# Two transformer blocks in exact-split fp32 on one core: activations streamed as hi and lo side by side, and the delta rule run in steps between weight products

## The chip, the cores and the metric

The kernel runs on one core of one Trainium2 chip. The metric is device time in microseconds, the median of several executions. The engines are named as in the profile: PE (TensorE matmul), PEld (its weight loads), DVE (VectorE), ACT (ScalarE), POOL (GpSimd) and SP (SyncE, which issues most transfers).

## What is computed

The input is x, 256 tokens by 2048 features. Two blocks of different kinds follow each other, each with weight matrices of 2048 rows and more, in float32:

```python
# first block
h = rms_norm(x, ln1[l])
proj = h @ w_in[l]                       # 11280 columns, split below
qkv_a, beta_a, decay_a, z_a, qkv_b, gate_a, gate_b = split_columns(proj)
y_a = gated_deltanet(qkv_a, beta_a, decay_a, z_a, ...) @ w_branch_a[l]
q_b, k_b, v_b = jnp.split(qkv_b, 3, axis=-1)     # rope on q and k, then attention
y_b = moba_attention(q_b, k_b, v_b).reshape(B, S, MOBA_WIDTH) @ w_branch_b[l]
x = x + (sigmoid(gate_a) * y_a + sigmoid(gate_b) * y_b) @ w_out[l]
u = causal_dwconv(rms_norm(x, ln2[l]) @ w_up[l], ffn_conv[l], ffn_conv_bias[l])
x = x + (silu(u_gate) * u_val) @ w_down[l]
# second block
z = h @ w_in[0]                          # pool columns, and r, k, v and lora columns
x = x + concat([pool_out, rwkv_out]) @ w_out[i]
x = x + jnp.square(jax.nn.relu(h2 @ w_ffn_up[i])) @ w_ffn_down[i]
x = x + sigmoid(rms_norm(x, ple_norm[i]) @ w_ple_gate[i]) * (p[i] @ w_ple_proj[i])
```

`gated_deltanet` is a recurrence over chunks of 64 tokens for 8 heads; the second block has another of the same kind (rwkv) for 16 heads of 64.

## The kernel before

Every product is made of three: an operand is split into hi (its value in the fp32r type that PE multiplies fast) and lo (the rest), and hi by hi, lo by hi and hi by lo are summed in PSUM. `load_w` fetches 512 KB of a weight matrix (raw) on SP's queue, ACT makes hi of it (L307) and DVE lo (L308); raw, hi and lo have three buffers each. The activations lie with features on partitions (`Norm.h`, `Norm.l`, tiles xh and xl, 16 slices of 128 features by 256 tokens).

`group_steps` computes 512 output columns: for each of the 16 slices and each half of the tokens, xh or xl is the stationary operand and 512 columns of the weight stream past it:

```python
mm(p, xh, h[:, j], start=(k == 0), stop=False, skip_group_check=True)    # L331
mm(p, xl, h[:, j], start=False, stop=False, skip_group_check=True)       # L332
mm(p, xh, l[:, j], start=False, stop=last, skip_group_check=True)        # L333
```

The result has tokens on partitions. Where the next step needs features on partitions, `turned_steps` has ACT evacuate it into u, times the norm's factor r (L368), and `feature_major` turns it by eight 128 x 128 transposes on PE (L249) for 512 columns; `take` then reads the turned tile in PSUM. So are computed: gdn_proj (q, k, v of the delta rule, 6 groups of 512 columns), q and k of the attention (4 groups, after a rotation by POOL along the row), up1 (22 groups), the lora columns (288), r, k, v and the pool columns of the second block (8 groups) and up2 (16 groups). The merge in branch_b is turned too. All other products (z, the gates, v, the branches, w_out, w_down) are used with tokens on partitions.

The order within an engine is that in which the program is written, shifted by a scheduler that works from its own model of the times; each engine then takes its instructions strictly in that order. In the first block the program text runs gdn_proj(0), z_proj(0), gdn_half(0), gdn_proj(1), z_proj(1), gdn_half(1), then attention. `gdn_half` is a chain: scales (L516), `gdn_pre` (L537 to L557), `inverse16`, which passes through DRAM and gives Z, `inverse64` and the rest of the inverse (L673 to L706), and `gdn_post` for two pairs of heads (L573 to L612). In the second block the chain of rwkv yields after each step, and `run` takes a number from a hand-written table after each and pulls so many units of other projections (`fill`) into the text there; a step of a projection costs 1.8 units.

PSUM has four one-bank tiles pp for the products, two of them for a group, and four tiles ps for the rest.

## Time and profile before

| what | value |
|---|---|
| median of three runs | 2911.91 us (2908.76 to 2915.29) |
| profiled execution, its own time | 2914.03 us |
| its span, first to last instruction | 2912.3 us |
| PE busy | 2818.7 us, 97%, 14224 instructions |
| DVE busy | 1698.9 us, 58% |
| ACT busy | 1391.3 us, 48% |
| POOL busy | 162.5 us, 6% |
| mean granted clock of PE | 0.976 |
| moved by DMA | 487.72 MB, mean 167 GB/s |

A busy share counts the time in which an engine has an instruction in flight. Matmuls overlap each other, so for PE the distance between the starts of two of them tells what one costs, and its duration doesn't. The granted clock is a share of 2.4 GHz; PE has two levels, 2.4 and 1.2 GHz, and a value between them is a mean over a stretch.

### The profile page before, as it was taken

To read this page: it belongs to the slowest core of one execution; us is meant where nothing else is said; L and a number is where in the kernel's file an instruction comes from. 1 tells how busy PE (TensorE), PEld (TensorE's weight loads), DVE (VectorE), ACT (ScalarE), POOL (GpSimd) and SP (SyncE) were. 2 spreads that over 40 slices of the span, in tenths; PEclk is the share of its full clock that TensorE was granted. 3 is DMA by queue.
4 is the path that set the end of the run, shared out by engine and by line. 5 is a ranking of instruction groups with operands and counts; after the bars stand their busy time and mean duration, and the time that the engine had idled before them with its cause. 6 is when DMAs were issued, how large, how long until landed. Compare 5 with 4: busy or idle time off the path is not lost.

```text
span 2912.3 us, 37683 instructions
## 1 busy us (share of the span) xinstructions
PE 2818.7 (97%) x14224; PEld 2298.8 (79%) x14224; DVE 1698.9 (58%) x2599; ACT 1391.3 (48%) x2062; POOL 162.5 (6%) x225
## 2 busy tenths in 40 slices
PE   9988989999999999999999999979999999999997
PEld 7867868888888888888887677766888888888886
DVE  6556656555556664665566595765645444454555
ACT  6535445444455544554455644423543443434454
POOL 0000100000000000000001031120010000100001
PEclk9988989999999999999999999988999999999999
DMA  7543535666566666666655454342565656666554
GB/s 214 168 121 102 164 102 170 180 190 185 182 184 186 184 187 189 187 182 187 203 179 176 133 141 131 104 123 73 152 186 187 188 184 188 185 187 201 182 181 152
DMA packets 281499, 487.72 MB, mean 167 GB/s; under 512 B 36442, under 2 KB 51813, under 8 KB 281317
## 3 DMA queue, kind: packets, MB, share of 16 engines
q1 hardware_dynamic: 280533, 482.94, 55.8%
q8 instruction: 111, 1.82, 0.3%
q10 hardware_dynamic: 608, 2.11, 0.2%
q14 instruction: 71, 0.58, 0.1%
q0 software_dynamic: 176, 0.27, 0.1%
HBM read 479.22 MB, written 6.03 MB: 167 GB/s over the span
## 4 chain that ended last, share of the span: by engine, by line
PE 90%; DVE 5%; DMA 2%; issue 1%; POOL 1%; ACT 1%; SPq 0%; ACTq 0%; DVEq 0%; POOLq 0%
PE pp L331 27%; PE pp L333 27%; PE pp L332 27%; PE ps L249 2%; DVE lo L308 2%; DMA s<-Ei 0%; PE ps L680 0%; DVE L L1082 0%; POOL X L664 0%; DMA Z<-s 0%; PE ps L1148 0%; PE ps L1150 0%; POOL pool L1231 0%; DMA raw<-in_w_in_dram 0%; PE ps L1160 0%
## 5 line engine op out<-in xcount | busy, mean ns | idle before, releaser
L308 DVE TENSOR_TENSOR lo<-raw,hi 128x1024 fp32r<-128x1024 f32 (+2 forms) x905 | 1113.4, 1231 | 982.3 <-ACT hi L307 927.1
L307 ACT ACTIVATE hi<-raw 128x1024 fp32r<-128x1024 f32 (+2 forms) x905 | 953.3, 1054 | 1097.4 <-PE pp L332 996.7
L331 PE MATMUL pp<-hi,xh 128*128 128x512 f32 (+1 forms) x2368 | 924.0, 390 | 2.6 <-ACT hi L307 2.0
L332 PE MATMUL pp<-hi,xl 128*128 128x512 f32 (+1 forms) x2368 | 923.2, 390 | 0.0
L333 PE MATMUL pp<-lo,xh 128*128 128x512 f32 (+1 forms) x2368 | 865.3, 390 | 8.1 <-DVE lo L308 7.9
L333 PEld LDWEIGHTS pp<-lo,xh 128*128 128x128 f32 x2368 | 445.4, 189 | 99.5 <-DVE lo L308 11.9
L331 PEld LDWEIGHTS pp<-hi,xh 128*128 128x128 f32 x2368 | 447.0, 189 | 94.2 <-issue 3.0
L332 PEld LDWEIGHTS pp<-hi,xl 128*128 128x128 f32 x2368 | 447.1, 189 | 88.7 <-issue 2.3
L332 PE MATMUL pp<-hi,hid 128*128 128x512 f32 x864 | 342.4, 397 | 0.0
L331 PE MATMUL pp<-hi,hid 128*128 128x512 f32 x864 | 342.1, 397 | 0.0
L333 PE MATMUL pp<-lo,hid 128*128 128x512 f32 x864 | 313.2, 397 | 0.0
L332 PEld LDWEIGHTS pp<-hi,hid 128*128 128x128 f32 x864 | 162.6, 188 | 39.6 <-DVE hid L380 0.5
L331 PEld LDWEIGHTS pp<-hi,hid 128*128 128x128 f32 x864 | 162.6, 188 | 38.9
L333 PEld LDWEIGHTS pp<-lo,hid 128*128 128x128 f32 x864 | 162.5, 188 | 38.7 <-DVE lo L308 0.2
L895 DVE SCALAR_TENSOR_TENSOR cva<-ps,PT,cva 128x255 f32<-128x255 f32 (+1 forms) x176 | 79.4, 477 | 2.1 <-ACT cva L892 1.0
L368 ACT ACTIVATE u<-pp,rstd 128x512 f32<-128x512 f32 (+1 forms) x74 | 49.9, 680 | 56.5 <-PE pp L333 49.7
L249 PE MATMUL ps<-C,u 128*128 128x128 f32 x486 | 73.8, 280 | 0.6 <-ACT u L368 0.6
L1322 POOL TENSOR_TENSOR u<-u 128x512 f32<-128x512 f32 x32 | 40.6, 1269 | 595.6 <-ACT u L1321 595.6
L249 PEld LDWEIGHTS ps<-C,u 128*128 128x128 f32 x486 | 61.7, 144 | 14.5 <-ACT u L368 1.0
L270 POOL TENSOR_TENSOR junk<-x,rows 128x512 f32<-128x512 f32 x8 | 12.3, 1536 | 1087.9 <-ACT junk L267 1087.9
L864 DVE TENSOR_TENSOR x<-x,pp 128x512 f32<-128x512 f32 x96 | 65.2, 686 | 4.8 <-PE pp L333 3.6
L331 PE MATMUL pp<-hi,mh 128*128 128x512 f32 x128 | 51.0, 398 | 0.0
(426 smaller groups left out, 2322.2 us busy)
## 6 DMA issues: line engine op xcount, KB each, us to landing
raw<-in_w_in_dram SPq DMA_DIRECT2D x240, 512.0 KB
raw<-in_w_up_dram SPq DMA_DIRECT2D x176, 512.0 KB
raw<-in_w_ffn_up_dram SPq DMA_DIRECT2D x128, 512.0 KB
raw<-in_w_ffn_down_dram SPq DMA_DIRECT2D x128, 512.0 KB
raw<-in_w_down_dram SPq DMA_DIRECT2D x88, 512.0 KB
raw<-in_w_out_dram SPq DMA_DIRECT2D x64, 512.0 KB
raw<-in_w_ple_gate_dram SPq DMA_DIRECT2D x32, 512.0 KB
raw<-in_w_branch_a_dram SPq DMA_DIRECT2D x16, 512.0 KB
```

The lines of the kernel that those rows point to most:

```text
L249: nc.tensor.transpose(p[:w, m - m0, i * 128:(i + 1) * 128], src[:, i, 128 * m:128 * m + w], ident)
L270: nc.gpsimd.tensor_tensor(out=y, in0=s, in1=self.w2[j], op=ALU.mult)
L307: act(h, r, AF.Copy)
L308: tt(out=l, in0=r, in1=h.bitcast(F32), op=ALU.subtract)
L331: mm(p, xh, h[:, j], start=(k == 0), stop=False, skip_group_check=True)
L332: mm(p, xl, h[:, j], start=False, stop=False, skip_group_check=True)
L333: mm(p, xh, l[:, j], start=False, stop=last, skip_group_check=True)
L368: act(u[:, i, :ncol], p, AF.Copy, scale=r()[:, i:i + 1])
L864: tt(out=s, in0=s, in1=p, op=ALU.add)
L895: stt(a[:, s:], p[:, :T - s], prm("ffn_conv", 88 * j + f), a[:, s:], ALU.mult, ALU.add)
L1322: nc.gpsimd.tensor_tensor(out=u[:, i], in0=u[:, i], in1=u[:, i], op=ALU.mult)
```

## The change

It has two parts. First, `wide_steps` takes the place of `turned_steps` and of `group_fm_steps`: the weight is the stationary operand, and hi and lo of the activations lie side by side in one tile xhl, so that one matmul streams 512 columns (256 tokens of hi, 256 of lo) past 128 columns of the weight's hi, and a second one streams the 256 columns of hi past the weight's lo. The result has features on partitions, 256 of them in one pass; raw holds four slices of 256 columns in place of two of 512. At the end of a pass ACT copies the part that came from lo to z, DVE adds the other part from PSUM and multiplies by the factor, which `spread` has turned into a row for all partitions. The rotation of q and k works along partitions, by a shuffle on DVE and three POOL operations. up2 squares on DVE instead of POOL. The pp tiles are two of two banks.

Second, `Fill` holds projections that are yet to be computed. The steps of `gdn_half` and of the attention heads yield numbers of units, and so many units of products are put between them: z and the second half's projections beside the first half of the delta rule, the attention's projections beside the second, gates and branch_a beside the heads. The second block's `pull` uses the same class: a step of `wide_steps` counts 1.0, one of `group_steps` 2.0 for 512 columns; the table of numbers is as it was.

```diff
-    pp = ctx.enter_context(tc.tile_pool(name="pp", bufs=4, space=bass.MemoryType.PSUM))
+    pp = ctx.enter_context(tc.tile_pool(name="pp", bufs=2, space=bass.MemoryType.PSUM))
...
+    def spread(col):
+
+        p2 = psum()
+        for i in range(2):
+            nc.tensor.transpose(p2[:, i * 128:(i + 1) * 128], col[:, i:i + 1].to_broadcast([128, 128]), ident)
+        rb = tm("rstd", T, bufs=1)
+        act(rb, p2[:, :T], AF.Copy)
+        return rb
...
-            self.h = cpool.tile([128, KT, T], F32R, tag="xh", name=nm("xh"))
-            self.l = cpool.tile([128, KT, T], F32R, tag="xl", name=nm("xl"))
+            self.hl = cpool.tile([128, KT, 2, T], F32R, tag="xhl", name=nm("xhl"))
...
+                        mm(P[:w, m].rearrange("p a b -> p (a b)"), h[:, j, f], x2.rearrange("p a b -> p (a b)"),
+                           start=(k == 0), stop=False, skip_group_check=True)
+                        mm(P[:w, m, 0], l[:, j, f], x2[:, 0], start=False, stop=last, skip_group_check=True)
+                        if not (last and m == len(ws) - 1):
+                            yield 1.0
+            w, nw = ws[0], len(ws)
+            z = tm("z", (2, T), bufs=2)[:w, :nw]
+
+            act(z, P[:w, :nw, 1], AF.Copy)
+            tt(out=z, in0=P[:w, :nw, 0], in1=z, op=ALU.add)
+            if r is not None:
+                tt(out=z, in0=z, in1=r()[:w].unsqueeze(1).to_broadcast([w, nw, T]), op=ALU.mult)
+            for m in range(nw):
+                take(o0 // 128 + m, z[:, m])
+            yield 1.0
...
+        Z = inverse16([p[0][:, 0] for p in pre], 2)
+        yield 55
+        for _ in rounds(gdn_inverse(pre[m:m + 2], Z[:, m:m + 2]) for m in (0, 2)):
+            yield 6
         for m in (0, 2):
-            lockstep(gdn_post(4 * half + m + i, sc, pre[m + i]) for i in range(2))
+            for _ in rounds(gdn_post(4 * half + m + i, sc, pre[m + i]) for i in range(2)):
+                yield 5
...
+    z0, z1, g1, a0, a1 = z_proj(0), z_proj(1), gdn_proj(1), attn_proj(0), attn_proj(1)
+    fills.add(z0, g1, z1)
+    fills.pull(30)
+    fills.between(gdn_half(0))
+    fills.upto(z1)
+    fills.add(a0, a1)
+    fills.between(gdn_half(1))
+    fills.upto(a0)
+    fills.between(rounds(attn_head(h) for h in (0, 1)))
+    fills.between(rounds(attn_head(h) for h in (2, 3)))
+    fills.upto(a1)
+    ba = [branch_a(j) for j in range(4)]
+    fills.add(*ba)
+    fills.between(rounds(attn_head(h) for h in (4, 5)))
+    fills.between(rounds(attn_head(h) for h in (6, 7)))
+    fills.upto(ba[3])
...
+        def ev(m, p):
+            stt(p, p, 0.0, p, ALU.max, ALU.mult)
+            split(hh[:, m], hl[:, m], p)
+
+        wide(w_up, 512 * i, 512, xs, lambda: r5, ev)
```

In the changed file the products of `group_steps` are L345 to L347, those of `wide_steps` L373 and L375, lo is L320, and the chain of the delta rule has moved down: L673 is L729 there, L700 and L706 are L756 and L762, L573 is L622, L612 is L661.

On PE, in an up projection of the first block, products and the transposes of the group before stood so (pp is the group's PSUM tile, C the identity, u the evacuated group):

```order
L331 MATMUL pp_11622<-hi_11644,xh_6034 128x512
L332 MATMUL pp_11622<-hi_11644,xl_6035 128x512
L249 MATMUL ps_11582<-C_84,u_11433 128x128
L249 MATMUL ps_11601<-C_84,u_11433 128x128
L333 MATMUL pp_11622<-lo_11645,xh_6034 128x512
...
L331 MATMUL pp_11622<-hi_11662,xh_6034 128x512
L249 MATMUL ps_11582<-C_84,u_11433 128x128 x3
L249 MATMUL ps_11601<-C_84,u_11433 128x128 x3
L332 MATMUL pp_11622<-hi_11662,xl_6035 128x512
```

At the seam of two passes of the same projection there is now:

```order
L373 MATMUL pp_12328<-xhl_6318,hi_12397 128x512
L375 MATMUL pp_12328<-xhl_6318,lo_12398 128x256
L373 MATMUL pp_12436<-xhl_6318,hi_12439 128x512
L375 MATMUL pp_12436<-xhl_6318,lo_12440 128x256
...
L373 MATMUL pp_12436<-xhl_6318,hi_12461 128x512
L375 MATMUL pp_12436<-xhl_6318,lo_12462 128x256
```

The transposes are gone from PE's queue, and products of 512 and 256 columns alternate.

On DVE, at the end of the second group of an up projection (cva is the convolution's sum, sgq the gate), before:

```order
L308 TENSOR_TENSOR lo_10732<-raw_10729,hi_10731 128x1024
L895 SCALAR_TENSOR_TENSOR cva_10622<-ps_10617,PT_81,cva_10622 128x255
L895 SCALAR_TENSOR_TENSOR cva_10622<-ps_10617,PT_81,cva_10622 128x254
L906 TENSOR_TENSOR cva_10622<-cva_10622,sgq_10286 128x256
L308 TENSOR_TENSOR lo_10750<-raw_10747,hi_10749 128x1024
```

and now:

```order
L320 TENSOR_TENSOR lo_12376<-raw_12373,hi_12375 128x1024
L382 TENSOR_TENSOR z_12310<-pp_12221,z_12310 128x512
L384 TENSOR_TENSOR z_12310<-z_12310,rstd_7019 128x512
L320 TENSOR_TENSOR lo_12398<-raw_12395,hi_12397 128x1024
L958 SCALAR_TENSOR_TENSOR cva_12314<-z_12310,PT_81,cva_12314 128x255
L958 SCALAR_TENSOR_TENSOR cva_12321<-z_12310,PT_81,cva_12321 128x255
L958 SCALAR_TENSOR_TENSOR cva_12314<-z_12310,PT_81,cva_12314 128x254
L958 SCALAR_TENSOR_TENSOR cva_12321<-z_12310,PT_81,cva_12321 128x254
L969 TENSOR_TENSOR cva_12314<-cva_12314,sgq_12012 128x256
L320 TENSOR_TENSOR lo_12440<-raw_12437,hi_12439 128x1024
```

The two operations on z are new there, and stand between two lo.

On PE, at the delta rule's first half, from the end of the inverse to the first pair's post, before (aq, c, d, f and e are the chain's own tiles):

```order
L706 MATMUL ps_1461<-aq_1166,ivp_1452 64x64 x2
L706 MATMUL ps_1461<-aq_1195,ivp_1452 64x64 x2
L706 MATMUL ps_1468<-aq_1224,ivp_1459 64x64 x2
L706 MATMUL ps_1468<-aq_1253,ivp_1459 64x64 x2
L573 MATMUL ps_1475<-c_1175,aq_1166 128x128
L573 MATMUL ps_1479<-c_1204,aq_1195 128x128
L578 MATMUL ps_1483<-d_1477,f_1173 128x128
```

and now in the first half:

```order
L762 MATMUL ps_1821<-aq_1227,ivp_1794 64x64 x2
L375 MATMUL pp_2846<-xhl_96,lo_2894 128x256
L373 MATMUL pp_2846<-xhl_96,hi_2915 128x512
L762 MATMUL ps_1828<-aq_1268,ivp_1801 64x64 x2
...
L375 MATMUL pp_2951<-xhl_96,lo_2955 128x256
L373 MATMUL pp_2951<-xhl_96,hi_2954 128x512
L622 MATMUL ps_1882<-c_1198,aq_1189 128x128
L622 MATMUL ps_1886<-c_1236,aq_1227 128x128
```

and in the second half (oah is the first half's result, which branch_a multiplies):

```order
L347 MATMUL pp_4567<-lo_4601,oah_98 128x512
L729 MATMUL ps_3038<-X_3016,aq_2617 64x64 x4
...
L762 MATMUL ps_3276<-aq_2701,ivp_3249 64x64 x2
L762 MATMUL ps_3276<-aq_2746,ivp_3249 64x64 x2
L622 MATMUL ps_3328<-c_2626,aq_2617 128x128
L622 MATMUL ps_3332<-c_2671,aq_2662 128x128
L627 MATMUL ps_3348<-d_3330,f_2624 128x128
```

In the first half products now stand between the steps of the chain; in the second they stand ahead of it, and the inverse and most of post follow each other without them.

## Rows read from the trace of the kernel before

**Rows 1.** The page: busy time, share and instructions of each engine, and the chain that ended last by engine and line.

```profile
PE 2818.7 (97%) x14224; PEld 2298.8 (79%) x14224; DVE 1698.9 (58%) x2599; ACT 1391.3 (48%) x2062; POOL 162.5 (6%) x225
PE 90%; DVE 5%; DMA 2%; issue 1%; POOL 1%; ACT 1%; SPq 0%; ACTq 0%; DVEq 0%; POOLq 0%
PE pp L331 27%; PE pp L333 27%; PE pp L332 27%; PE ps L249 2%; DVE lo L308 2%; DMA s<-Ei 0%; PE ps L680 0%; DVE L L1082 0%; POOL X L664 0%; DMA Z<-s 0%; PE ps L1148 0%; PE ps L1150 0%; POOL pool L1231 0%; DMA raw<-in_w_in_dram 0%; PE ps L1160 0%
```

**Rows 2.** The timeline of PE in an up projection of the first block: start and length in us, engine, line, operation, names, shape, count. Between the first two rows eleven more products start; one product of L333 starts between the two transposes at 1188.97 and the row of 1189.42, and one of L332 between the six at 1190.35 and the row of 1191.24.

```profile
1185.80 0.39 PE L331 MATMUL pp<-hi,xh 128*128 128x512 f32 x1
...
1188.52 0.39 PE L331 MATMUL pp<-hi,xh 128*128 128x512 f32 x1
...
1188.97 0.38 PE L249 MATMUL ps<-C,u 128*128 128x128 f32 x2
...
1189.42 0.39 PE L331 MATMUL pp<-hi,xh 128*128 128x512 f32 x1
...
1190.35 0.82 PE L249 MATMUL ps<-C,u 128*128 128x128 f32 x6
...
1191.24 0.39 PE L333 MATMUL pp<-lo,xh 128*128 128x512 f32 x1
```

**Rows 3.** The page's group of PE's transposes of u: count, busy us and mean ns, idle time before them.

```profile
L249 PE MATMUL ps<-C,u 128*128 128x128 f32 x486 | 73.8, 280 | 0.6 <-ACT u L368 0.6
```

**Rows 4.** Windows of the instructions on pp alone (the products and their evacuations): stretch, its length, busy us and count on PE, PEld, DVE and ACT, the granted clock, DMA share and GB/s.

```profile
189.00:240.00 51.00, 0.69 (x3) 0.40 (x3) 0.00 (x0) 1.12 (x2) 0.67 0.13 35
1943.00:1954.00 11.00, 0.29 (x2) 0.00 (x0) 0.99 (x2) 0.00 (x0) 0.70 0.60 139
2027.00:2041.00 14.00, 0.00 (x0) 0.00 (x0) 0.00 (x0) 0.00 (x0) 0.50 0.00 0
```

**Rows 5.** Windows of all instructions, with POOL after ACT: a stretch of up projections of the first block, and one at the start of the second block's chain.

```profile
900.00:1040.00 140.00, 140.00 (x643) 116.01 (x642) 89.39 (x126) 80.09 (x115) 0.00 (x0) 1.00 0.64 185
1674.00:1747.00 73.00, 69.49 (x372) 55.29 (x371) 67.77 (x118) 33.58 (x59) 23.86 (x41) 1.00 0.53 143
```

**Rows 6.** Groups by line and shape on DVE and ACT: count, busy us, mean ns of one, idle time before them and what ended it.

```profile
L308 DVE TENSOR_TENSOR lo<-raw,hi 128x1024 fp32r<-128x1024 f32 x892 | 1104.1, 1239 | 975.7 <-ACT hi L307 920.7 <-PE ps L249 45.6 <-PE ps L573 3.2
L307 ACT ACTIVATE hi<-raw 128x1024 fp32r<-128x1024 f32 x892 | 944.9, 1060 | 1082.0 <-PE pp L332 982.8 <-issue 38.2 <-DMA raw<-in_w_in_dram 24.7
L848 DVE TENSOR_TENSOR u<-pp,sg 128x512 f32<-128x512 f32 x8 | 5.5, 692 | 0.1
L849 DVE TENSOR_TENSOR u<-u,mg 128x512 f32<-128x512 f32 x8 | 5.1, 683 | 0.0
L895 DVE SCALAR_TENSOR_TENSOR cva<-ps,PT,cva 128x255 f32<-128x255 f32 x88 | 40.2, 477 | 1.0 <-ACT cva L892 1.0
L234 DVE TENSOR_TENSOR tiny<-tiny 128x2 f32<-128x2 f32 x45 | 7.0, 160 | 0.7
L1082 DVE TENSOR_TENSOR L<-sw,E 64x256 f32<-64x256 f32 x16 | 13.0, 811 | 0.2
L1085 DVE TENSOR_TENSOR BK<-rk,Ei 64x256 f32<-64x256 f32 x16 | 8.1, 507 | 0.4
L417 ACT ACT_TABLE_LOAD x3 | 3.8, 1283 | 0.1
```

**Rows 7.** The timeline of PE at two places with products of 256 columns: the last gate (activations stationary), and pool_w of the second block (weights stationary; between its two rows three more products start).

```profile
2874.05 0.28 PE L332 MATMUL pp<-hi,xl 128*128 128x256 f32 x1
2874.17 0.28 PE L333 MATMUL pp<-lo,xh 128*128 128x256 f32 x1
```

```profile
1828.75 0.28 PE L354 MATMUL pp<-junk,hi 128*128 128x256 f32 x1
...
1829.22 0.28 PE L355 MATMUL pp<-dl,hi 128*128 128x256 f32 x1
```

**Rows 8.** The timeline of PE in w_down, where hid is stationary; between the two rows three more products start.

```profile
1508.84 0.40 PE L333 MATMUL pp<-lo,hid 128*128 128x512 f32 x1
...
1509.78 0.40 PE L331 MATMUL pp<-hi,hid 128*128 128x512 f32 x1
```

**Rows 9.** Windows of all instructions in the last gate: rows of 2 KB, then of 1 KB; the last two columns are the DMA share and GB/s.

```profile
2840.00:2860.00 20.00, 20.00 (x90) 16.57 (x89) 12.31 (x12) 10.33 (x14) 2.92 (x2) 1.00 0.62 193
2873.00:2883.00 10.00, 10.00 (x84) 9.96 (x83) 7.31 (x7) 6.47 (x10) 2.92 (x2) 1.00 0.55 168
```

**Rows 10.** The timeline of PE at the delta rule of the first block; in brackets the idle time before the row and what ended it.

```profile
200.99 2.34 PE L673 MATMUL ps<-X,aq 64*64 64x64 f32 x32 [11.55 <-POOL X L664]
...
239.75 0.78 PE L331 MATMUL pp<-hi,xh 128*128 128x512 f32 x1
```

```profile
341.06 0.68 PE L673 MATMUL ps<-X,aq 64*64 64x64 f32 x16
342.79 0.68 PE L673 MATMUL ps<-X,aq 64*64 64x64 f32 x16 [1.05 <-POOL X L664]
...
372.43 0.38 PE L573 MATMUL ps<-c,aq 128*128 128x128 f32 x2
```

```profile
378.07 0.75 PE L593 MATMUL ps<-c,aq 128*128 128x128 f32 x4 [0.72 <-DVE c L588]
...
400.23 0.80 PE L331 MATMUL pp<-hi,xh 128*128 128x512 f32 x1 [0.62 <-ACT u L736]
```

**Rows 11.** The same at the second half of the second block's chain.

```profile
1953.23 1.12 PE L673 MATMUL ps<-X,GB 64*64 64x64 f32 x16 [9.94 <-POOL X L664]
```

## Prediction before the run

> **What bounds the kernel now.** I read the page first: TensorE is busy 97% of the span, VectorE 58%, ScalarE 48%, and the chain that ended last is 90% PE, four fifths of it the three product lines L331 to L333 [rows 1]. A saturated engine is judged by the distance between starts, since each matmul's own 390 ns overlaps the next one. In the PE timeline of an up projection, twelve 512-column products start between 1185.80 and 1188.52 us, one every 0.227 us [rows 2]. With 484 of the small L249 transposes of u in this trace [rows 3], that is where this change acts. The windows then show the places where PE has next to no product to run: 189 to 240 us (0.69 us of product in 51 us, granted clock 0.67, a mix of the levels 1.2 and 2.4 GHz) and, in the second block, 1943 to 1954 and 2027 to 2041 [rows 4]. In the dense stretches the clock is 1.00 and VectorE is busy 64% [rows 5]: there only fewer or cheaper PE instructions shorten the time.
>
> **The transposes removed.** The page counts 486 under L249 with u; the 32 of the branch_b merge stay (4 column groups by 8), so 454 go: 48 of gdn_proj, 32 of the q and k projections, 176 of up1, 6 of the lora, 64 of rkv and pool, 128 of up2. In the timeline six of one batch and one product take from 1190.35 to 1191.24 us, 0.89; less the product (0.23) that is 0.66, or 0.110 each; the pair with a product from 1188.97 to 1189.42 gives 0.112 [rows 2]. PE is saturated there, so all of it counts: 454 x 0.111 = **-50.4 us**. Their evacuation u on ScalarE goes as well, off the path.
>
> **The products.** For 512 output features and one 128-row slice, before: six matmuls of 512 columns, 6 x 0.227 = 1.362 us. After: four of 512 and four of 256, with the same 3072 columns, but eight instructions. A 256-column product costs 0.120 us with the activations stationary and 0.11 to 0.12 with the weights stationary (L354 to L356) [rows 7]; I take 0.118. So 4 x (0.227 + 0.118) = 1.380, 0.018 more, by 16 slices and 56 groups: **+16.1 us**. The trace has no 512-column product with weights stationary and activations streaming. Its bounds: at 0.226 and 0.115 a slice costs 4 x 0.341 - 6 x 0.226 = 0.008 more, +7 us; products that hold hid stationary start 0.235 apart [rows 8], and 0.234 with 0.120 gives 0.054 more, +48 us. I stay at 0.227, because both operands come from the tiles that gave it (xh, hi). The lora's 288 columns become 128 + 128 + 32: 48 pairs of 0.345 = 16.6 us against 96 products that I estimate at 0.133 (between 0.120 for 256 and 0.227 for 512 columns), 12.8 us: **+3.8 us**. The gates and pool_w cost the same either way.
>
> By the Trainium skill, TensorE: Matmul & The Clock Gate, section Back-to-back issue gap, a warm matmul costs its columns at 2.4 GHz plus 2.5 ns, which would make eight instructions 4 ns dearer than six and this term an estimated +3.6 us, 12 less than mine. The rows speak against it here: 0.227 and 0.120 leave some 13 ns beside the columns [rows 2, 7].
>
> **Work that moves to VectorE.** Each pass of 256 features now ends with z: one ScalarE copy, one VectorE add from PSUM and one multiply by the factor (0.69 and 0.68 us, as L848 and L849 [rows 6]); the rows show every other operation as before. A pair of up1 groups gets 4 x 1.37 = 5.5 us more in 44 us; from 64% VectorE rises to some 77%. The order puts a lo between two short runs of these, the longest without a lo five operations of at most 0.48 us, 2.4 us. A raw slice is split when PE frees the buffer, two slices (2 x 2.76 us) ahead of need, less 1.06 for hi and 1.24 for lo [rows 6]: 3.2 us of slack. So I cost it at nothing; without that cover each of 114 passes would pay.
>
> **Transfers.** A weight load stays 512 KB but in rows of 1 KB. The stage that already has such rows shows share 0.55 at 168 GB/s against 0.62 at 193 GB/s [rows 9]: the same per byte, no cost. The eight transposes of spread stand behind 8 to 18 us of products, longer than the fourteen 0.16 us steps of the factor that they need [rows 6]; I put **+1 us** for the lot. Four more table loads of 1.28 us fall on ScalarE, which is half idle.
>
> **The delta rule of the first block.** Before, the first half runs with no product: PE stops at 189.4, waits 11.55 us for Z, runs the inverse and the two pairs of post, and meets the first product at 239.75: 50.3 us. The second half's inverse lies among 87 products: 341.1 to 372.4 is 31.4 us, of which 87 x 0.227 = 19.7 are products, so it costs 11.6; its post is bare again, 377.35 to 400.23 = 22.9 [rows 10]. Together 84.8 us beside the products. After, the order has 489 products between the first half's L729 and its last L661, so that half costs its own matmuls: 11.6 for the inverse, 36 x 0.11 = 4 for post, and I allow 2 for waits. But the fill runs dry in the second half: gate and the first quarter of branch_a stand ahead of L729, the rest of branch_a needs oah of this half, and only 13 products follow until the last L661. So the second half is what the first was, 200.99 to 239.75 = 38.8 us, and 1 us for Z (137 products cover that wait, 139 did it before with 1.05 left). 57.4 against 84.8: **-27 us**. Bounds: nothing, if the first half's steps wait as long among products as alone; and -40, if the bare half keeps the full clock: 0.67 means two thirds of the time at 1.2 GHz [rows 4], and if all of that were work it would take half, 13 us less.
>
> **The second block.** A projection was 33 steps at 1.8 = 59.4 units and is 64 now, with the same table of numbers: a unit buys 0.344 us of products instead of 0.366, and more is left for the second half. The order has 134 products (23.4 us) instead of 63 (14.3) ahead of its inverse, where PE waited 9.94 us for X [rows 4, 11]; and 203 instead of 120 from there to the end of the chain, where 2027 to 2041 was bare. I take 10 for the wait and 9 for the last steps. Against it stands VectorE, busy 67.8 of 73 us at 1674 [rows 5]: seven projections bring 7 x 2.7 = 19 us to it, of which I charge 5. **-14 us**; bounds +5 and -33.
>
> By the Trainium skill, SBUF — State Buffer, section Who interferes with whom, a VectorE instruction with two SBUF inputs waits for a GpSimd one that reads SBUF. The rows agree: one shape costs 811 ns at L1082, with GpSimd at work beside it, and 507 at L1085 [rows 6]. If all seven projections' multiplies were stretched by 1.6, VectorE would get an estimated 6 us more here.
>
> **Sum.** -50.4 + 16.1 + 3.8 + 1 - 27 - 14 = -70.5 us. The profiled execution took 2914.0 us, 2.1 above the median of the three runs; so 2843.5 on its own scale and **2841** on the median's.
>
> **Rivals.** (a) The products are dear, 0.234 and 0.120: +32, **2873**. For it: products on hid run so for no reason that the trace names [rows 8]; against it: those on xh don't [rows 2]. (b) The cheap ends: products 9 less and the second block -33: **2813**. For it: most of that block's bare time is waiting; against it: its VectorE. (c) The interleaving doesn't do what it says: PE takes its queue in order, a small matmul that waits holds the products behind it, and the first half gains nothing: +27, **2868**. Against it: the second half's inverse among products left only 1.05 us of wait. (d) The other side: z holds up lo. Its add stands in VectorE's queue ahead of the next lo and waits for PE's last product and ScalarE's copy; if the slack of 3.2 us is used up, PE stops at the end of each pass. From 70.5 / 114 = 0.62 us a pass it eats the gain; at 1.0 us, **2955**. For it: VectorE's load grows most of all; against it: it sits idle before lo, 921 of 976 us for ScalarE's hi, which itself waits for PE [rows 6]. (e) About the same as before, (d) near its point of balance.
>
> **Chances.** Forecast 0.46, (a) 0.13, (b) 0.18, (c) 0.13, (d) 0.07, (e) 0.03. Within 0.2% is what a measurement of this kernel can tell from no change; so faster 0.90, same 0.03, slower 0.07. The range leaves out (d), (e), a corner where (a) and (c) meet, and what lies under (b): 2798 to 2884.
>
> **What would show it.** Starts of the 512- and 256-column products near 0.227 and 0.118 apart; no L249 but spread's eight and the merge's; the first half's L729 to L661 full of products and one bare stretch of some 39 us before the attention heads; no wait over 2 us at the second block's second Z. PE waits for lo at ends of passes, or VectorE over 85% in up1, would prove (d); a distance of 0.234 proves (a).

## The result, and the profile after

| | before | after |
|---|---|---|
| median of four runs each | 2910.89 us | 2840.37 us (2839.50 to 2846.79) |
| ratio | | 0.9761, 95% interval 0.9742 to 0.9779 |
| span of the profiled execution | 2912.3 us | 2838.5 us |

The page of the kernel after: busy time of each engine, the chain that ended last by line, and the groups that answer to [rows 1, 3, 6].

```profile
PE 2773.4 (98%) x15538; PEld 2330.5 (82%) x15538; DVE 1856.4 (65%) x2908; ACT 1397.2 (49%) x2088; POOL 159.2 (6%) x217
PE pp L373 28%; PE pp L375 15%; PE pp L345 14%; PE pp L346 14%; PE pp L347 14%; DVE lo L320 1%; PE ps L261 1%; DMA Z<-s 1%; PE ps L736 0%; DVE L L1143 0%; PE ps L1209 0%; PE ps L729 0%; PE ps L1211 0%; POOL X L720 0%; DMA s<-Ei 0%
L320 DVE TENSOR_TENSOR lo<-raw,hi 128x1024 fp32r<-128x1024 f32 x902 | 1109.1, 1230 | 809.5 <-ACT hi L319 789.5
L373 PE MATMUL pp<-xhl,hi 128*128 128x512 f32 x3648 | 1292.9, 398 | 2.0 <-DVE z L382 2.0
L375 PE MATMUL pp<-xhl,lo 128*128 128x256 f32 x3648 | 1031.7, 283 | 1.9 <-DVE lo L320 1.9
L382 DVE TENSOR_TENSOR z<-pp,z 128x512 f32<-128x512 f32 (+2 forms) x119 | 80.8, 679 | 1.3 <-ACT z L381 1.1
L384 DVE TENSOR_TENSOR z<-z,rstd 128x512 f32<-128x512 f32 x114 | 78.3, 688 | 3.3
```

PE is still what bounds the kernel. In all 3648 pairs PE waited 2.0 us for z and 1.9 for lo, and z's two operations took 0.68 and 0.69 us: rival (d) is nowhere. No transpose of u is left on PE.

The timeline of PE in the kernel after, at four places. Between the first two rows lie 15 pairs (a product of L373 and one of L375), between the next two 12 products of the first block's w_down, where hid is stationary; then again 15 pairs, and 12 products of the second block's w_down.

```profile
899.80 0.39 PE L373 MATMUL pp<-xhl,hi 128*128 128x512 f32 x1
...
905.00 0.39 PE L373 MATMUL pp<-xhl,hi 128*128 128x512 f32 x1
...
1049.64 0.39 PE L345 MATMUL pp<-hi,hid 128*128 128x512 f32 x1
...
1052.44 0.39 PE L345 MATMUL pp<-hi,hid 128*128 128x512 f32 x1
...
1149.91 0.40 PE L373 MATMUL pp<-xhl,hi 128*128 128x512 f32 x1
...
1155.21 0.40 PE L373 MATMUL pp<-xhl,hi 128*128 128x512 f32 x1
...
2149.78 0.39 PE L345 MATMUL pp<-hi,hid 128*128 128x512 f32 x1
...
2152.53 0.39 PE L345 MATMUL pp<-hi,hid 128*128 128x512 f32 x1
```

A pair costs 5.20 / 15 = 0.347 us at 900 and 5.30 / 15 = 0.353 at 1150, where 0.345 was forecast. Products on hid, 0.235 before [rows 8], are 0.233 and 0.229 apart: a gain that no term of the sum had.

Windows of the instructions on pp alone in the kernel after: the stretch of [rows 4], then the chain of the delta rule's first half and of its second. Columns as there.

```profile
189.00:240.00 51.00, 43.23 (x210) 35.03 (x209) 1.36 (x2) 2.41 (x4) 1.00 0.61 165
213.00:322.00 109.00, 96.81 (x494) 78.23 (x492) 4.11 (x6) 4.72 (x8) 1.00 0.56 158
399.00:442.00 43.00, 7.66 (x19) 4.54 (x18) 0.00 (x0) 1.27 (x2) 0.76 0.19 57
```

The first half (from its first L729 at 213.66, which waits for nothing, to the end of its last L661 at 321.9) is full of products; the second, 399.7 to 441.4, is bare. Taking 13.5 ns beside a product's columns at 2.4 GHz, the 489 products of the first half are 90.0 us of 108.3, so its own steps cost 18.2 us (forecast 17.6); the second half has 14 products, and its own steps cost 38.5 (forecast 38.8 and 1 for Z). Counted in the same way, the steps before cost 38.1 us in the first half, after the wait of 11.55, and 36.8 in the second. The clock has a part in this: the bare stretch of 51 us at 189 was granted 0.67 before [rows 4], the filled first half 1.00 now, the bare second half 0.76. How much of the gain is the clock and how much is waiting that products cover was not separated.

The same stages cut out of each trace, each from a product on one tile to a product on a later one, show where the time went; the runs of the next section stand beside. (The first row is called the first mixer below; the last 117 us, alike in all traces, are left out.) The last columns are the kernel after with transposes put back (on the shared tiles, and on a tile of their own), before with a tile of its own, and after with aligned tiles.

| stage, us | before | after | order alone | wide alone | put back, shared | put back, own | before, own | aligned |
|---|---|---|---|---|---|---|---|---|
| start to branch_b's first product on obh | 616.2 | 576.5 | 609.5 | 586.2 | 617.5 | 588.9 | 605.4 | 574.8 |
| branch_b and w_out | 206.0 | 204.4 | 204.6 | 204.4 | 204.4 | 204.4 | 206.1 | 202.1 |
| up1 and w_down | 749.8 | 742.1 | 744.9 | 742.1 | 757.2 | 757.2 | 750.5 | 736.8 |
| second block to its last w_out product | 495.8 | 483.8 | 492.9 | 489.6 | 490.8 | 496.4 | 501.2 | 488.3 |
| up2 and w_down | 727.7 | 714.6 | 725.6 | 714.6 | 725.8 | 726.5 | 728.1 | 713.1 |
| median of the runs | 2910.9 | 2840.4 | 2893.0 | 2855.9 | 2914.7 | 2892.6 | 2911.7 | 2833.4 |

The dense stages repeat to 0.1 us where the code is the same. The second block doesn't: it took 480.5 to 504.2 us in the traces of the changed kernel and its variants, so a few us there tell nothing.

### The profile page after: what moved, and what is told of

It is laid out like the page before. It is cut to its first block, busy times and chain, and to the rows that moved or that the text cites. A ratio compares the mean times of both kernels' runs of the same rounds, so it can differ in the third digit from the quotient of the medians.

```text
span 2838.5 us, 40515 instructions
## 1 busy us (share of the span) xinstructions
PE 2773.4 (98%) x15538; PEld 2330.5 (82%) x15538; DVE 1856.4 (65%) x2908; ACT 1397.2 (49%) x2088; POOL 159.2 (6%) x217
## 4 chain that ended last, share of the span: by engine, by line
PE 91%; DVE 5%; DMA 1%; ACT 1%; issue 1%; POOL 1%; SPq 0%; ACTq 0%; POOLq 0%; DVEq 0%
PE pp L373 28%; PE pp L375 15%; PE pp L345 14%; PE pp L346 14%; PE pp L347 14%; DVE lo L320 1%; PE ps L261 1%; DMA Z<-s 1%; PE ps L736 0%; DVE L L1143 0%; PE ps L1209 0%; PE ps L729 0%; PE ps L1211 0%; POOL X L720 0%; DMA s<-Ei 0%
## 5 line engine op out<-in xcount | busy, mean ns | idle before, releaser
L320 DVE TENSOR_TENSOR lo<-raw,hi 128x1024 fp32r<-128x1024 f32 x902 | 1109.1, 1230 | 809.5 <-ACT hi L319 789.5
L319 ACT ACTIVATE hi<-raw 128x1024 fp32r<-128x1024 f32 x902 | 953.4, 1057 | 1200.6 <-PE pp L346 563.8
L373 PE MATMUL pp<-xhl,hi 128*128 128x512 f32 x3648 | 1292.9, 398 | 2.0 <-DVE z L382 2.0
L375 PE MATMUL pp<-xhl,lo 128*128 128x256 f32 x3648 | 1031.7, 283 | 1.9 <-DVE lo L320 1.9
L373 PEld LDWEIGHTS pp<-xhl,hi 128*128 128x128 f32 x3648 | 684.9, 188 | 164.8 <-DVE z L382 2.4
L375 PEld LDWEIGHTS pp<-xhl,lo 128*128 128x128 f32 x3648 | 689.7, 189 | 9.9 <-issue 4.7
L345 PE MATMUL pp<-hi,hid 128*128 128x512 f32 x864 | 340.0, 394 | 0.0
L347 PE MATMUL pp<-lo,hid 128*128 128x512 f32 x864 | 339.4, 393 | 0.0
L347 PE MATMUL pp<-lo,xhl 128*128 128x512 f32 (+1 forms) x544 | 206.4, 379 | 0.0
L346 PE MATMUL pp<-hi,xhl 128*128 128x512 f32 (+1 forms) x544 | 206.2, 379 | 0.0
L345 PE MATMUL pp<-hi,xhl 128*128 128x512 f32 (+1 forms) x544 | 205.9, 378 | 0.0
L347 PEld LDWEIGHTS pp<-lo,hid 128*128 128x128 f32 x864 | 162.2, 188 | 37.0
L345 PEld LDWEIGHTS pp<-hi,hid 128*128 128x128 f32 x864 | 162.2, 188 | 36.1
L345 PEld LDWEIGHTS pp<-hi,xhl 128*128 128x128 f32 x544 | 102.4, 188 | 18.6
L346 PEld LDWEIGHTS pp<-hi,xhl 128*128 128x128 f32 x544 | 102.4, 188 | 18.4
L347 PEld LDWEIGHTS pp<-lo,xhl 128*128 128x128 f32 x544 | 102.4, 188 | 18.2
```

Of the source, the lines that this page charges most:

```text
L319: act(h, r, AF.Copy)
L320: tt(out=l, in0=r, in1=h.bitcast(F32), op=ALU.subtract)
L373: mm(P[:w, m].rearrange("p a b -> p (a b)"), h[:, j, f], x2.rearrange("p a b -> p (a b)"), start=(k == 0), stop=False, skip_group_check=True)
L375: mm(P[:w, m, 0], l[:, j, f], x2[:, 0], start=False, stop=last, skip_group_check=True)
```

## Experiments

**Order alone.** The changed kernel's order with the products of before: `wide_steps` computes groups of 512 columns and turns them.

```diff
-                        mm(P[:w, m].rearrange("p a b -> p (a b)"), h[:, j, f], x2.rearrange("p a b -> p (a b)"),
...
+        yield from group_steps(W, 0, ops, c0, ncol, ev, before)
+        feature_major(u, ncol, take)
```

> The new order alone: projections computed as before (activations stationary, the result turned by eight transposes a group), with the changed kernel's order and its units of products between the steps of the delta rule. The run with the transposes put back showed the first mixer at 617.5 us against 576.5, as long as before (616.2), although its text has the new order. Theory now: the turned tiles take their PSUM tiles ps in turn with the chain's, so a projection can't run ahead of the chain, whatever the text says; the order alone then gives nothing in the first mixer, some 10 us on hid and mh by the changed places in memory, and up to 10 in the second block: 2890 to 2905 us. Rival, the prediction's: the order is what fills the first half, 25 to 32 us besides: 2860 to 2870 us.

Measured: 2893.0 us, ratio to before 0.9929 (0.9916 to 0.9943). The first mixer gained 6.7 us. PE first waits 14.01 us for Z; then 289 products do stand in the first half, but its steps still cost 33.4 us beside them, the 24 transposes among them included. An earlier version of this run, for which 2860 us was expected (the order worth 32), did not fit into SBUF and gave no time.

**Wide products alone.** The first block's text in the old sequence, without `Fill`.

```diff
-    fills.add(z0, g1, z1)
-    fills.pull(30)
-    fills.between(gdn_half(0))
...
+    drain(z_proj(0), gdn_half(0), gdn_proj(1), z_proj(1), gdn_half(1))
+    drain(attn_proj(0), *[attn_head(h) for h in range(4)])
```

> The wide products alone in the first block: there the text runs in the old sequence (z and first half, second projection and second half, attention, heads, branch), with no units of products put between the steps; the second block and all products as in the changed kernel. If the parts add up, the bare first half comes back: 50 us in place of 18.8 us beside its products, and the second half loses its bare 38.9 for some 34: 2840 + 27 = 2867 us, between 2862 and 2875. Rival, the scheduler finds the same interleaving without the text's help: 2840 to 2846 us.

Measured: 2855.9 us, 0.9809 (0.9788 to 0.9831), between what was expected and what the rival said. Windows of the instructions on pp in this run, at the first half of the delta rule and beside the attention heads:

```profile
215.00:323.00 108.00, 96.08 (x489) 77.86 (x489) 4.11 (x6) 4.72 (x8) 1.00 0.55 157
439.00:586.00 147.00, 129.87 (x539) 102.32 (x539) 5.14 (x8) 4.18 (x7) 0.96 0.52 154
```

The first half is as full as in the kernel after, 489 products, though no unit of the text puts any there: once the transposes are gone, the scheduler finds them. What the text's order adds is 9.7 us of the first mixer, of which most lies beside the heads (from the last L661 to branch_b 146.9 us here, 135.2 in the kernel after, for the same 538 products).

**Transposes put back.** After each pass, four transposes of z into a PSUM tile that nothing reads, 454 in all; first from the tiles ps, then from a tile of their own, with three ps left.

```diff
+            if r is not None:
+                pj = psum((2, T))
...
+                        nc.tensor.transpose(pj[:, m, i * 128:i * 128 + wm], z[:wm, m, i * 128:(i + 1) * 128],
+                                            ident[:wm, :wm])
```

```diff
-                pj = psum((2, T))
+                pj = pj1.tile([128, 2, T], F32, tag="pj", name=nm("pj"))
```

> The removed transposes by themselves: after each pass PE transposes its z (four of 128 by 128 a pass, 454 in all as before) into a PSUM tile that nothing reads; all else as in the changed kernel. By the prediction's 0.111 us each: 50.4 us more, 2891 us. By the stages of the two traces, where the removed transposes account for 43.8 us of starts, 0.096 each: 2884 us. If they would only fill time in which PE waits in any case: under 10 us more.

> The changed kernel with the 454 transposes put back as before, but into a PSUM tile of their own (one bank), with three tiles ps left for all else. Theory: put back among the tiles ps they cost 74 us, of which 0.088 us each in the dense up projections (40 us in all) are their work on PE and the rest is the fill that they hold back by taking ps in turn with the delta rule's chain; with a tile of their own the first half is filled again and 34 us come back: 2880 us, 2875 to 2890. Rival, it is PE's strict order that holds the fill back, a transpose that waits for z standing ahead of products: 2905 to 2915 us as with shared tiles. Three tiles in place of four for the chain may cost some us in either.

Measured: 2914.7 us (1.0006, 0.9996 to 1.0015), no gain left, and far more than any size that was expected; with a tile of their own 2892.6 (0.9929, 0.9915 to 0.9942), just above the range. The first mixer took 617.5 and 588.9 us, against 576.5 in the kernel after: where results that nothing reads are put is worth 28.6 us there.

**Before, with a tile of its own.** The kernel before, its text and products untouched, its turned results in a PSUM tile of their own.

```diff
-            p = psum((2, T))
+            p = pj1.tile([128, 2, T], F32, tag="pj", name=nm("pj")) if own else psum((2, T))
```

> The kernel before, in its own order and with its own products, with one thing changed: the results that are turned go into a PSUM tile of their own, and three tiles ps are left for the rest. Theory: what left the delta rule's first half bare was that the turned results took the tiles ps in turn with the chain; with a tile of their own the scheduler fills the half from the old text, as it does in the run with wide products alone, and the first mixer shrinks from 616 by about 21 us, the wait of 11.55 us for Z with it; the second block's wait of 9.94 may go too: 2880 to 2895 us. Rival, the evacuation through the single tile u, or the wide form, is needed for that: 2905 to 2915 us.

Measured: 2911.7 us, 0.9996 (0.9987 to 1.0005). The total went the rival's way, though the first half was filled as the theory had it. The chain's first product of the first half (64 x 64, aq) in the timelines of four runs, with the idle time before it: order alone, put back on shared tiles, put back on its own tile (here the second batch; the first had no wait), and before with its own tile, whose second half follows.

```profile
203.89 2.35 PE L725 MATMUL ps<-X,aq 64*64 64x64 f32 x32 [14.01 <-POOL X L716]
```

```profile
199.47 1.81 PE L735 MATMUL ps<-X,aq 64*64 64x64 f32 x22 [12.85 <-POOL X L726]
```

```profile
223.54 0.68 PE L736 MATMUL ps<-X,aq 64*64 64x64 f32 x16 [0.45 <-POOL X L727]
```

```profile
227.74 0.68 PE L674 MATMUL ps<-X,aq 64*64 64x64 f32 x16 [0.81 <-POOL X L665]
...
417.26 2.34 PE L674 MATMUL ps<-X,aq 64*64 64x64 f32 x32 [9.48 <-POOL X L665]
```

On shared tiles PE waits for Z as long as before (11.55 us, [rows 10]), whether the text has the new order or not; with a tile of their own it doesn't, in the old text too. So it is the turned results, taking the tiles ps in turn with the chain's, that kept products from covering this wait: shown. PE's strict order, the rival's reason in the expectation above, is not needed for it, since the own tile leaves the transposes in PE's queue. The steps behind the wait are less clear: put back on shared tiles they cost 23.3 us beside 352 products, with order alone 33.4 beside 289, on an own tile 20.4 (put back) and 21.2 (before), the transposes included each time; why order alone is the dearest stays open. In the kernel before, the own tile alone shortens the first mixer by 10.8 us, not 21, since the wait comes up again at the second half (9.48 us, 1.05 before). The total shows nothing: the second block was 5.4 us longer in this trace, which is within its scatter.

**One more operation on z.**

```diff
+                tt(out=z, in0=z, in1=z, op=ALU.max)
```

> One more VectorE operation on z in each pass (the maximum of z with itself, 512 columns, two operands in SBUF, at 0.69 us as the multiply of z): 114 times, 78 us of VectorE, in the place that the rival (d) of the prediction speaks of, ahead of the next lo. If z is hidden behind a slack of about 3 us, as the prediction has it, nothing moves in the dense stretches: 2840 us in the up projections, and at most 3 us more in the second block, where VectorE is nearly full: up to 2846 us. If z holds up lo in part already, each pass pays its 0.69 us: 2918 us, or half of it, 2880 us.

Measured: 2834.9 us, 0.9730 (0.9716 to 0.9745). Windows of all instructions at 900 to 1000 us, of the kernel after and of this one:

```profile
900.00:1000.00 100.00, 100.00 (x579) 88.16 (x578) 75.14 (x107) 57.34 (x81) 0.00 (x0) 1.00 0.61 190
```

```profile
900.00:1000.00 100.00, 100.00 (x579) 88.15 (x578) 80.11 (x116) 57.40 (x81) 0.00 (x0) 1.00 0.62 190
```

VectorE goes from 75 to 80%, and PE starts the same 579 products. Both FFN stages kept their length to 0.1 us: z isn't only hidden, it has room for another 0.69 us a pass. That the median is 5 us under the kernel after's is no gain of this operation: the profiled execution took 2840.0 us, and the other executions scatter down to 2831.9.

**The second block's table at its old rate.**

```diff
-        fills.pull(n)
+        fills.pull(n * 64 / 59.4)
```

> Only the second block's rate of filling: each number of its table times 64/59.4, so that a step of the chain pulls as large a part of a projection as before the change (a projection has 64 units now and had 59.4). By the prediction's step, that less is pulled early and more is left for the second half, the wait for the second half's X (9.94 us before, 1.5 now) comes back at least in part and the end of the chain is barer: 4 to 12 us more, 2845 to 2852 us. Rival, the second block gained by its products and the order does not hang on the rate: within 2 us of 2840.

Measured: 2846.0 us, four runs from 2831.9 to 2856.6; 0.9773 (0.9749 to 0.9798). The longest wait at the second half's Z in this run (for BK; X was waited for no longer than 0.55 us), and one stretch of all instructions in this run and in the kernel after:

```profile
1929.01 0.94 PE L729 MATMUL ps<-BK,GB 64*64 64x64 f32 x16 [1.52 <-POOL BK L720]
```

```profile
1574.00:1618.00 44.00, 44.00 (x100) 25.25 (x100) 11.48 (x15) 16.73 (x31) 0.00 (x0) 0.50 0.17 49
```

```profile
1574.00:1618.00 44.00, 44.00 (x225) 31.64 (x225) 24.08 (x40) 24.29 (x42) 1.95 (x3) 1.00 0.39 110
```

The wait of 9.94 us [rows 11] stays away at the old rate too, so the rate isn't what removed it. The time, though in the range expected, tells nothing either way: this execution ran 44 us at 1.2 GHz, long before this wait, and started 100 matmuls in them where the kernel after, at 2.4, started 225.

The wait for X at the same place with the transposes put back on shared tiles, with order alone, and in the kernel before with a tile of its own:

```profile
1958.12 0.68 PE L735 MATMUL ps<-X,GB 64*64 64x64 f32 x16 [2.81 <-POOL X L726]
```

```profile
1940.46 1.12 PE L725 MATMUL ps<-X,GB 64*64 64x64 f32 x16 [6.80 <-POOL X L716]
```

```profile
1982.48 1.12 PE L674 MATMUL ps<-X,GB 64*64 64x64 f32 x16 [9.26 <-POOL X L665]
```

All three traces with the products of before have it (9.94, 6.80, 9.26 us); in the eleven with wide products no wait there is over 2.81.

**Products for the bare second half.** Two gates (22 us of products each) are given slots in which they can leave PSUM early, and put among the fill of the second half; in a second run one of them is held until the inverse has ended.

```diff
-        dst = sg[j] = halves(Q(7, name="sg"))
+        dst = sg[j] = halves(Q(slot, name="sg"))
...
-    fills.add(a0, a1)
+    fills.add(a0, a1, ga[0], ga[1])
```

```diff
+        if hold:
+            nc.vector.tensor_copy(P[:, 0, :1], hold[0])
```

> Two gates of 22 us of products are put among the fill of the delta rule's second half, and the tiles are exchanged so that they can leave PSUM there (the gates' tile sg takes the slot of the first half's z, free by then, and a spare one; the heads' result obh takes the slot that sg had). In the order 32.5 us of products then stand between the second half's first L729 and its last L661, where 3.4 us stand in the changed kernel. Theory: the second half is bare only because a gate could not leave PSUM before the chain freed its slot; its steps cost 38.9 us bare and cost 18.8 us beside products in the first half, so 12 to 20 us go: 2820 to 2828 us. Rival, the steps wait as long among the products, or the products are missed later beside the attention heads: 2836 to 2842 us.

> Two gates as in the run with gates ahead, with the same exchange of tiles; the first covers the wait for Z, and the second is held until the inverse of the second half has ended (its PSUM tile is first written by a copy of one column from the inverse's result), so that its 22 us of products stand between the steps of the second half's post. The run with both gates ahead put them among the inverse, which has no idle time to fill (11 us bare, all work), and left post bare: 28 us beside its products with 8 us idle and 14 to 20 us at the lower clock. Theory: beside products post costs some 8 us as in the first half, so 10 to 18 us go: 2823 to 2831 us. Rival, the time is only moved to the attention heads, which then lack these products: 2838 to 2844 us.

Measured: 2843.0 (0.9768, 0.9755 to 0.9780) and 2849.2 us (0.9793, 0.9768 to 0.9818); the first mixer took 577.6 and 579.1 us, against 576.5. Windows of pp in the first of the two, over inverse and post, and in the second the wait for X and the last wait of post:

```profile
400.00:432.00 32.00, 23.32 (x95) 17.26 (x94) 0.00 (x0) 1.25 (x2) 1.00 0.46 141
432.00:470.00 38.00, 15.87 (x51) 10.30 (x52) 0.00 (x0) 0.00 (x0) 0.82 0.28 82
```

```profile
399.21 2.35 PE L736 MATMUL ps<-X,aq 64*64 64x64 f32 x32 [5.27 <-POOL X L727]
...
464.63 0.74 PE L663 MATMUL ps<-C,e 128*128 128x128 f32 x2 [3.95 <-DVE e L659]
```

Both times the second half's own cost stayed (37.0 us beside its products, and 36.8 with the wait for X, against 38.5). First the products fell into the inverse, which had next to no idle time to fill; then, spread over post, they were missing at Z. The products that need nothing of the chain are used up by then: the rival, time that is only moved, is right.

**Places in memory.** The tiles hid, mh, oah and obh are moved by unused pads, or the weights' tiles hi and lo are.

```diff
+    pad0 = tmp.tile([128, 16], F32, tag="pad0", name="pad0", bufs=1)
...
+    pad1 = quad.tile([128, 56], F32, tag="pad1", name="pad1", bufs=1)
```

(24 columns in the second pad for the shifted run, 56 for the aligned one; for the weights' tiles one pad of 16 columns behind raw.)

> Two unused pads of 64 and 96 bytes a partition, so that the tiles hid, mh, oah and obh begin at the same place within 128 bytes (32) as xhl, hi and lo; in the changed kernel they begin at 96 or at 0, and before the change at 64 or at 0. Nothing else is different. Theory: the place within 128 bytes of the stationary tile sets the distance of products, 0.2267 us at 32, 0.229 at 96, 0.2333 at 0 or 64; then all products on hid, mh, oah and obh start 0.2267 apart, and some 3500 products gain 11 to 13 us: 2828 us. Rival, the distance goes with what is multiplied and not with where it lies: 2840 us, hid at 0.229 to 0.233 as before.

> One unused pad of 64 bytes behind the raw weights, so that hi and lo begin at 96 within 128 bytes in place of 32, while xhl stays at 32; hid and the like move to 64 or stay at 32 (second block). If the place of the stationary tile alone sets the distance, the wide products (hi stationary) start 0.349 to 0.353 us a pair apart and products on xhl stay at 0.2267: some 5 to 10 us more, 2845 to 2850. If the distance goes with the difference between the stationary and the streamed tile, the products on xhl (now 64 apart) go to 0.229 as well and hid in the second block (32 against 96) stays at 0.229. If neither counts, 2840.

> The pads of the shifted run again, the second one larger by 128 bytes, so that hid, mh, oah and obh all begin at the same place within 256 bytes (160) as xhl, hi and lo. Read from the runs so far, by the stationary tile's place less the streamed one's within 256 bytes: products start 0.2267 us apart at 0, 0.229 at 192, 0.232 at 128, 0.2333 to 0.234 at 224, 160 and 96. Theory: that difference sets the distance, so w_down of the first block goes from 0.2326 to 0.2267 a product (1056 of them, 6 us less) and that of the second from 0.2293 to 0.2267 (1536, 4 us less), with 2 us from obh and mh: FFN stages of 736 and 711 us and 2828 us in all. Rival, the shifted run's second block hit 0.2267 by chance of another cause: the first block's w_down stays near 0.2315, 2836 us.

Measured: shifted 2840.6 us (0.9780, 0.9754 to 0.9806), weights shifted 2858.1 (0.9828, 0.9811 to 0.9846), aligned 2833.4 (0.9730, 0.9717 to 0.9743). Timelines of PE, 18 products between the two rows of each place: w_down of the first and of the second block in the shifted run, then in the aligned one; last, with the weights shifted, 15 pairs, and 15 products of the last gate with xhl stationary.

```profile
1049.66 0.40 PE L349 MATMUL pp<-hi,hid 128*128 128x512 f32 x1
...
1053.85 0.39 PE L349 MATMUL pp<-hi,hid 128*128 128x512 f32 x1
...
2149.65 0.39 PE L349 MATMUL pp<-hi,hid 128*128 128x512 f32 x1
...
2153.73 0.39 PE L349 MATMUL pp<-hi,hid 128*128 128x512 f32 x1
```

```profile
1049.63 0.39 PE L349 MATMUL pp<-hi,hid 128*128 128x512 f32 x1
...
1053.71 0.39 PE L349 MATMUL pp<-hi,hid 128*128 128x512 f32 x1
...
2149.74 0.39 PE L348 MATMUL pp<-hi,hid 128*128 128x512 f32 x1
...
2153.82 0.39 PE L348 MATMUL pp<-hi,hid 128*128 128x512 f32 x1
```

```profile
900.24 0.40 PE L376 MATMUL pp<-xhl,hi 128*128 128x512 f32 x1
...
905.54 0.40 PE L376 MATMUL pp<-xhl,hi 128*128 128x512 f32 x1
...
2770.17 0.39 PE L348 MATMUL pp<-hi,xhl 128*128 128x512 f32 x1
...
2773.61 0.39 PE L348 MATMUL pp<-hi,xhl 128*128 128x512 f32 x1
```

In the shifted run the two blocks' tiles share their place within 128 bytes but not within 256: 0.2328 and 0.2267 us. Aligned within 256 bytes both are at 0.2267, and the first block's FFN stage falls by 5.3 us, the second's by 1.5. The theory of 128 bytes was wrong, that of 256 held. With the weights shifted the products on xhl go to 0.229, though xhl stayed where it was: the place of the stationary tile alone doesn't set the distance. The pairs, 64 bytes apart there, are at 0.353 throughout, and the run is slower than any expectation for it: 7.9 us more in the two FFN stages than the kernel after, the rest in the mixers. Of the 7 us that the aligned median gains on the kernel after, 6.8 are read in the two FFN stages; the rest of the trace (2.3 less in branch_b, 1.7 less in the first mixer, 4.5 more in the second block) is partly scatter.

## Why the prediction was right

The forecast was 2841, the time 2840.4. The direction was right, and so were the places where time would go; the cause of two terms was not, and that the total hits within 1 us is luck, since terms that were off by 6 to 13 us cancel.

**Transposes: -50.4 forecast, -44 read.** Start to start, the removed ones leave 15.5 us in up1, 11.3 in up2, and 8.6 and 8.4 in the two mixers. That is 0.088 each in the dense stages, as the run with their own tile nearly gives back (15.1 us for 176), and not 0.111: the two batches of [rows 2] were dearer than the mean.

**Products: +19.9 forecast with the lora, +26 read.** Up1's went from 483.3 to 493.5 us, up2's from 351.7 to 358.6, the first mixer's from 480.2 to 481.1, the second's from 313.8 to 321.9. A pair measured 0.347 to 0.353 us and not 0.345, and the products before 0.229 on average in these stages and not 0.227. By the Trainium skill (TensorE: Matmul & The Clock Gate, Back-to-back issue gap) a warm matmul takes its columns at 2.4 GHz plus 2.5 ns; two more instructions a slice are 5 ns by that and the term without the lora an estimated 4.5 us (the prediction's 4 ns and 3.6 us are a slip). The trace disagrees: 13 to 20 ns stand beside the columns of a product (0.2267 to 0.2333 us for 512).

**A term that was missing: -12.7.** Products on hid, mh and ml got cheaper (247.7 to 245.4, 360.7 to 351.9, 90.2 to 88.6), because the change moved their tiles: the aligned run shows that the place decides. The prediction had seen 0.235 beside 0.227 and named no reason [rows 8]. These three errors, 6, 6 and -13, cancel.

**z and lo.** Nothing, as forecast; shown with one more operation of the multiply's length. The 6 us by which the prediction's estimate lets GpSimd stretch the multiplies in the second block aren't there either: of the 17 with 512 columns in that stage none took over 0.70 us.

**The delta rule of the first block: -27 forecast, -32 read, and for another cause.** The first mixer lost 39.7 us; less 8.6 of transposes and plus 0.9 of products, 32 are left. By the count of 13.5 ns a product, some 28 of them are the wait for Z and the two halves (86.4 us beside the products before, 56.7 after, 1.4 of the difference for 16 transposes), and some 5 lie beside the attention heads, where the prediction put nothing. The picture was right (first half full, second bare, 39 us), but the step that gave it to the interleaved text failed. The text's order by itself gives 6.7 us: that is close to what rival (c) said, but not for its reason, since with the same strict queue of PE and a tile of their own for the turned results the wait is covered. The wide products give 30.0 us without the new order, some 22 of them apart from the transposes' own time. The cover came from a side effect of the removed transposes, that their results no longer take the tiles ps in turn with the chain, which the prediction didn't weigh at all. Read as the prediction had it, the order could have been had without the wide products for some 27 us; on the shared tiles it can't. The new order with the products of before and a tile of their own for the turned results was not run, so how much of the 32 us needs the wide products stays open.

**The second block: -14 forecast, -12 read.** Its cause failed too: the fewer products for a unit are not what removed the wait for X. Nor are the transposes by themselves (2.81 us with them put back) or the tiles that they share (9.26 in the kernel before with a tile of its own); with the order alone it was 6.80. The wait goes with the form of the products; by what of that form stays open, as does the whole size, since this block varies by more than that.

## What to carry

Ask of an operation that is removed not only what it costs on its engine but which buffers it holds: 80 transposes in the first mixer were worth 9 us of PE time, but put back they cost 41 where they shared rotating PSUM tiles with a slow chain, and 12 with a tile of their own. Independent work can be spent once: when all of it is used up, a better place for it only moves the bare stretch. Where products of one shape differ by a few ns between stages, look at where their tiles begin; two pads of 64 and 224 bytes took 6.8 us off two stages and gave the lowest median here, 2833.4 us (though the run with one more operation on z came to 2834.9 by the second block's scatter).

## What the hardware showed that was not expected

In these traces the distance of 512-column products whose stationary operand is an activation goes with the place of the stationary tile less that of the streamed one, within 256 bytes (places from the addresses of the built kernels): 0.2267 us at 0, 0.229 at 192, 0.233 at 128 (a mean), 0.2333 at 224, 0.2333 to 0.235 at 160 and 96; other differences were not read. At 192 it was read with hid at 96 and hi at 160, and, with the weights shifted, with hid or xhl at 160 and hi at 224, all within 256 bytes; at 224 with hid at 128 and hi at 160, and at 192 and 224: it is the difference that counts. The wide pair has a second level that this doesn't explain: with one and the same places it ran at 0.347 us in some stretches and 0.353 in others, each for hundreds of products (with the weights moved by 64 bytes, always at 0.353); what decides between them stays open. And two of the profiled executions (the old rate's, and the second of those with gates ahead) spent 44 and 41 us from about 1575 us on at 1.2 GHz, in products mixed with small matmuls of the second block and with no idle time on PE, where in the others at most 10 us of that stretch ran so. In the run with the second gate held, the two executions with a mean granted clock of 0.978 and 0.979 took 2863.2 and 2867.2 us, the three with 0.985 took 2847.9 to 2849.2; what decides stays open.
